# A decoder layer in float32 on one core: TensorE's moving operands read in turn from two halves

## The chip, the cores and the metric

The kernel runs on one core of a Trainium2 chip. The metric is the device time of one execution in microseconds (us); before the change the median of three runs is 2019.43 us (2018.99 to 2019.73). The engines of the core work side by side and wait for each other through semaphores: TensorE (PE in the profile; its weight loads are shown as PEld), VectorE (DVE), ScalarE (ACT), GpSimd (POOL) and SyncE (SP), which here issues the weights' DMAs.

## The reference

One decoder layer on 256 tokens, model width 2048, in float32. Both branches read the same normalized input, and a gated sum of them is projected and added to `x`; a convolutional FFN follows.

```
h = rmsnorm(x, attn_norm_w[l])
proj = h @ w_in[l]
z, xbc, dt_raw, q, k, v, g = split(proj)              # 2048 -> 4096, 6144, 64, 3 x 2048, 4096
y_ssm  = ssd_mixer(z, xbc, dt_raw, ...) @ w_ssm_out   # conv of 4 tokens, 64 heads of 64, 8 groups, state 128
y_attn = moba_attention(q, k, v, ...) @ w_attn_out    # 16 heads of 128; one block of 256, so causal attention
g_ssm, g_attn = split(sigmoid(g + b_gate))
x = x + (g_ssm * y_ssm + g_attn * y_attn) @ w_out
h = rmsnorm(x, ffn_norm_w[l])
u = causal_dwconv(h @ w_up[l], ffn_conv_w, ffn_conv_b)  # 2048 -> 2 x 5632, conv of 3 tokens
u_gate, u_up = split(u)
x = x + (silu(u_gate) * u_up) @ w_down[l]
```

## The kernel before

All weights (about 95 million numbers) are read once from HBM, 1 MB at a time (`unit`, a tile of 128 x 2048 named `wraw`, three buffers, SyncE's queue). To keep float32 accuracy each operand of a product is split into two parts: the high part, rounded to the type float32r that TensorE takes, and the low part, the rest. ScalarE makes the high part of the weights (`whi`, L182), VectorE the low one (`wlo`, L183); each 1 MB gives two such pairs of 128 x 1024. Activations are kept split likewise, transposed, with the channels on the partitions and the 256 tokens in the free dimension: `hp` (input of attention and its gates), `hn` (normalized input of the SSD branch), `ot` (attention output), `yt` (SSD output), `mt` (merged), `fh` (FFN input), `a` (FFN middle). Each is a tile of 128 x 2 x 16 x 256; index 0 and 1 of the second dimension are high and low part.

A product takes three matmuls for each 128 x 128 piece of the weights: high weight with high activation (L215), high weight with low activation (L216), low weight with high activation (L218). This is `cm_chunk`; `cm_unit` makes one output block of 128 channels x 256 tokens out of 48 such matmuls, in one PSUM tile `mm` of four. The weights are the stationary operand, which TensorE loads anew for each matmul; the activation's 256 columns are the moving operand, streamed through. Only the value projection has it the other way round (`tm_chunk`, L376, L377, L382: `hp` is stationary, 512 columns of the weights `wv` move), since values are needed with the tokens on the partitions. Its weights are laid out by `_tm` on the host.

The stages in order: values and `hp` (`tm_units`); queries and keys of 16 heads in pairs, with attention between them (`attn_pair`); attention gates (`gate_attn`, L614) and attention output (L672); the SSD branch in eight groups (`group_units`, then `core_steps`, of which `ydot` has the matmuls L840 and L841 with moving tile `mhl`, and the reads L843, L845, L846 of their PSUM tile `cc`), SSD gates (`gate_ssm`) and SSD output projection (`out_unit`, added up in `yacc`, L894 and L896, a part of `slotA`); merging (`merge`, L947); output projection (L976 to L978); FFN up (`up`, L1013 reads PSUM) and down (`down`, L1038) in three parts. The attention and SSD steps of vectors are spread among the matmul units by `Spread.tick`: a unit's matmuls, then some steps. TensorE's order is that in which the code is written; the other engines' order follows the code as well. Smaller things on TensorE are sums over partitions (L287, L325), transposes (L544 to L546, L793), scores and B-C products (L228 to L230, L515, L516) and probabilities with values (L561 to L564).

The tiles of the split activations begin at addresses that padding tiles (`pad0`, `pad1` and others) set.

Of the kernel before, what the change touches and what calls it, by code (L numbers as in the profile page):

```python
# [8 lines left out]
F32 = mybir.dt.float32  # L9
# [54 lines left out]


def _tm(w, c0, n):
    v = w[:, c0:c0 + n * 512].reshape(4, 4, 128, n, 512).transpose(3, 0, 2, 1, 4)
    return np.ascontiguousarray(v).reshape(n, 4, 128, 2048)


# [50 lines left out]

class Spread:
# [34 lines left out]
def _body(tc, nc, d, out):  # L161
# [48 lines left out]

    def cm_chunk(ps, part, xh, xl, k0, nk, first, last):
        hi, lo = part
        for k in range(nk):
            w = hi[:, k * 128:(k + 1) * 128]
            PE.matmul(ps, w, xh[:, k0 + k], start=first and k == 0, stop=False)  # L215
            PE.matmul(ps, w, xl[:, k0 + k], start=False, stop=False)  # L216
        for k in range(nk):
            PE.matmul(ps, lo[:, k * 128:(k + 1) * 128], xh[:, k0 + k], start=False, stop=last and k == nk - 1)  # L218

    def cm_unit(src, xh, xl, nk=16):  # L220
        parts = unit(src, nk * 128)
# [148 lines left out]
    def tm_chunk(pst, part, k0, first, last):  # L370
        hi, lo = part
        for k in range(2):
            wh = hi[:, k * 512:(k + 1) * 512]
            for tt in range(2):
                ts = slice(tt * 128, (tt + 1) * 128)
                PE.matmul(pst[tt], hph[:, k0 + k, ts], wh, start=first and k == 0, stop=False)  # L376
                PE.matmul(pst[tt], hpl[:, k0 + k, ts], wh, start=False, stop=False)  # L377
        for k in range(2):
            wl = lo[:, k * 512:(k + 1) * 512]
            for tt in range(2):  # L380
                ts = slice(tt * 128, (tt + 1) * 128)
                PE.matmul(pst[tt], hph[:, k0 + k, ts], wl, start=False, stop=last and k == 1)  # L382


    def tm_units(srcs, after_unit, before=None, mid=None):
# [58 lines left out]
    def attn_pair(j):  # L444
        st = {}

        def evac(key, h, ps):
            if h == 0:
                st["n" + key] = ap.tile([128, 2, T], F32, name="n" + key, bufs=2)
                st["s" + key] = ap.tile([128, 2, T], F32, name="sq", bufs=2)  # L450
            S.activation(st["s" + key][:, h], ps, AF.Square)
            S.activation(st["n" + key][:, h], ps, AF.Copy, scale=sm("qn") if key == "q" else kscale)

        def sums(key):
            def f():
# [154 lines left out]
    def gate_attn(o, pg=None):  # L610
        if pg is None:
            pg = cm_unit(d["wga"][o], hph, hpl)
        g = gate_half(o)
        V.tensor_tensor(g, pg, rb, op=MUL)  # L614
        if o >= 6:
            gate_sigmoid(o, g)
        return g
# [22 lines left out]
    def hn_steps():  # L640
        xr = {}

        def load(c):
            def f():
                xr[c] = xb.tile([128, 4, T], F32, name="xr", bufs=2)
                nc.gpsimd.dma_start(xr[c], d["xT"][:, 4 * c:4 * c + 4])
            return f

        def norm(c):
            def f():  # L650
                x = xr.pop(c)
                for k in range(4):
                    V.scalar_tensor_tensor(x[:, k], x[:, k], sm("attn_w", 4 * c + k), rb, op0=MUL, op1=MUL)
                ks = slice(4 * c, 4 * c + 4)
                S.activation(hnh[:, ks], x, AF.Copy)
                V.tensor_tensor(hnl[:, ks], x, hnh[:, ks].bitcast(F32), op=SUB)
            return f

        return [[load(0), load(1)], [], [norm(0), load(2)], [], [norm(1), load(3)], [], norm(2), [], norm(3)]

    sp.add(hn_steps(), 18)
    for o in range(KT):
        if o > 6:
            gl[o] = gate_attn(o)
            sp.tick()
        elif o < 6:
            gate_sigmoid(o, gl[o])
        if o == 3:
            gl[6] = gate_attn(6, pg6)
        po = cm_unit(d["wao"][o], oh_, ol_)  # L670
        g = gl.pop(o)
        V.tensor_tensor(g, g, po, op=MUL)  # L672
        if o % 2:
            nc.gpsimd.dma_start(ma[o // 2], gpair.pop(o // 2))
        sp.tick()
# [19 lines left out]
    def dt_unit():  # L695
        raw = base.tile([128, 2048], F32, name="wraw", bufs=3)
        nc.sync.dma_start(raw[:, :1024], d["wdt"])
        rv = raw[:, :1024].rearrange("p (k c) -> p k c", c=64)
        ps = mm_tile()[:, :T]
        for c in range(2):  # L700
            w = base.tile([128, 1024], F32R, name="whi", bufs=3).rearrange("p (k a c) -> p k a c", a=2, c=64)
            ks = slice(8 * c, 8 * c + 8)
            S.activation(w[:, :, 0], rv[:, ks], AF.Copy)
            V.tensor_tensor(w[:, :, 1], rv[:, ks], w[:, :, 0].bitcast(F32), op=SUB)
            for k in range(8):
                wk = w[:, k].rearrange("p a c -> p (a c)")
                PE.matmul(ps, wk, hnh[:, 8 * c + k], start=c == 0 and k == 0, stop=False)
                PE.matmul(ps, wk, hnl[:, 8 * c + k], start=False, stop=c == 1 and k == 7)
        return ps

    def dt_steps(ps):
# [48 lines left out]
    def core_steps(g):  # L760
# [73 lines left out]
        def ydot(p):  # L834
            def f():
                m = st.pop(("m", p))
                for h in range(2):
                    ps = c_tile().rearrange("p (a t) -> p a t", t=T)
                    x0, x1 = [st["x"][:, s, p, 2 * h:2 * h + 2].rearrange("p a c -> p (a c)") for s in range(2)]
                    PE.matmul(ps, x0, m[:, :, h, 0:256], start=True, stop=False)  # L840
                    PE.matmul(ps[:, :, 128:], x1, m[:, :, h, 256:384], start=False, stop=True)  # L841
                    rs, ls = slice(h * 64, (h + 1) * 64), slice(64 - h * 64, 128 - h * 64)
                    V.scalar_tensor_tensor(yz[rs, p], pr[rs, 4 + p], sm("ssm_d", 4 * g + p, 1, rs), ps[rs, 0],  # L843
                                           op0=MUL, op1=ADD)
                    V.tensor_tensor(yz[rs, p], ps[rs, 1], yz[rs, p], op=ADD)  # L845
                    V.tensor_tensor(yz[rs, p], ps[ls, 0], yz[rs, p], op=ADD)  # L846
                if p % 2:
                    V.tensor_tensor(yz[:, p - 1:p + 1], yz[:, p - 1:p + 1], pr[:, p - 1:p + 1], op=MUL)
            return f
# [32 lines left out]
    def out_unit(q, u, done):  # L882
        parts = unit(d["wso"][q, u])
        yh, yl = yt[:, q % 2, 0], yt[:, q % 2, 1]
        ps = mm_tile()
        for c in range(2):
            cm_chunk(ps[:, c * T:(c + 1) * T], parts[c], yh, yl, 0, 8, True, True)
        done(u, ps.rearrange("p (a t) -> p a t", t=T))

    def acc_done(q):  # L890
        def f(u, ps):
            y = yacc[:, 2 * u:2 * u + 2]
            if q == 0:
                S.activation(y, ps, AF.Copy)  # L894
            else:
                V.tensor_tensor(y, ps, y, op=ADD)  # L896
        return f
# [37 lines left out]
    def merge(u, ps):  # L935
        os_ = slice(2 * u, 2 * u + 2)
        if u < 4:
            g = gate_pool.tile([128, 2, T], F32, name="g", bufs=3)
            nc.gpsimd.dma_start(g, gs[u])
            late = pre[0][:, 2 * u:2 * u + 2]  # L940
            with tc.issue_after(last_rsq[0].ins):
                S.activation(late, late, AF.Sigmoid)
        else:
            g = pre[0][:, 2 * u - 8:2 * u - 6]
        a = gate_pool.tile([128, 2, T], F32, name="g", bufs=3)
        nc.gpsimd.dma_start(a, ma[u])
        V.tensor_tensor(yacc[:, os_], ps, yacc[:, os_], op=ADD)  # L947
        V.tensor_tensor(yacc[:, os_], yacc[:, os_], g, op=MUL)
        V.tensor_tensor(a, yacc[:, os_], a, op=ADD)
        S.activation(mh_[:, os_], a, AF.Copy)  # L950
        V.tensor_tensor(ml_[:, os_], a, mh_[:, os_].bitcast(F32), op=SUB)
# [21 lines left out]
            yield o, pss[o] if o < 2 else cm_unit(d["wout"][o], mh_, ml_)  # L973

    for o, ps in out_products():
        V.tensor_tensor(x1[:, o], ps, x1[:, o], op=ADD)  # L976
        S.activation(fh[:, o], x1[:, o], AF.Copy, scale=sm("ffn_w", o))
        V.scalar_tensor_tensor(fl[:, o], x1[:, o], sm("ffn_w", o), fh[:, o].bitcast(F32), op0=MUL, op1=SUB)  # L978
        if o == 0:
            S.activation(ssum, x1[:, o], AF.Square)  # L980
        else:
# [45 lines left out]
    def down(th):  # L1027
        at = acts[th]
        n = thirds[th][1]
        for o in range(KT):  # L1030
            ps = cm_unit(d[wd[th]][o], at[:, 0], at[:, 1], n)
            if th == 2 and o == KT - 1:
                for h, q in enumerate((S, nc.sync)):
                    hs = slice(h * 128, (h + 1) * 128)
                    V.tensor_tensor(x1[:, o, hs], ps[:, hs], x1[:, o, hs], op=ADD)
                    q.dma_start(out[o][:, hs], x1[:, o, hs])
                continue
            V.tensor_tensor(x1[:, o], ps, x1[:, o], op=ADD)  # L1038
            if th == 2:
                S.dma_start(out[o], x1[:, o])  # L1040

# [29 lines left out]
```

## Time and profile before

| | |
|---|---|
| median of three runs | 2019.43 us (2018.99 to 2019.73) |
| profiled execution, from first to last instruction | 2017.6 us |
| TensorE busy | 2012.3 us, 17203 matmuls |
| VectorE busy | 1496.5 us |
| ScalarE busy | 1189.5 us |
| DMA | 402.40 MB, mean 199 GB/s |

The profiled execution's own time is known as its span alone; the median of the runs is 1.8 us above it. In the profile's rows the columns are, for groups of instructions: line, engine, operation, output tile and inputs, shape, count, then busy time in us, mean duration of one in ns, and the idle time before them. For rows in order of time: start in us, duration in us, engine, line, operation, count in a row. Durations of matmuls overlap, so what one costs is read from the distance of starts.

### The profile page before, as it was taken

Reading aid. Unit: us, or ns where it says so; the run is one execution under the profiler, and the core shown is the slowest. Engines: PE = TensorE matmul, PEld = TensorE weight load, DVE = VectorE, ACT = ScalarE, POOL = GpSimd, SP = SyncE. Lnnn points to the kernel's source line nnn. Section 1 sums busy time; section 2 is a strip of 40 time slices with the busy share of each in tenths; the row PEclk is TensorE's granted clock in tenths of the full one; section 3 lists DMA queues with packets and bytes.
Section 4 is the critical chain, followed back from the end, with each engine's and each line's share of the span. In section 5 each row is a group of like instructions: output and inputs, shape, how many; then the busy total and the mean of one; then the engine's idle time right before and its main releaser. Section 6 shows DMA issues by size and latency. Waiting matters only on the chain.

```text
span 2017.6 us, 40769 instructions
## 1 busy us (share of the span) xinstructions
PE 2012.3 (100%) x17203; PEld 1989.1 (99%) x17203; DVE 1496.5 (74%) x2214; ACT 1189.5 (59%) x1640; POOL 79.0 (4%) x100
## 2 busy tenths in 40 slices
PE   9999999999999999999999999999999999999999
PEld 7999999999999999999999999999999999999999
DVE  7588877656788798888989886677777765677554
ACT  6466655544768867667677645565555553455333
POOL 0012210000000000000000000000000000000000
PEclk9999999999999999999999999999999999999999
DMA  7555555656556555555565575555555555555555
GB/s 290 188 187 183 181 177 206 234 204 215 188 192 217 205 199 208 194 196 190 196 208 178 197 276 200 190 189 198 199 189 191 201 194 189 194 201 190 190 186 169
DMA packets 64351, 402.40 MB, mean 199 GB/s; under 512 B 7655, under 2 KB 10264, under 8 KB 20648
## 3 DMA queue, kind: packets, MB, share of 16 engines
q1 hardware_dynamic: 55384, 376.56, 52.9%
q0 software_dynamic: 5760, 18.97, 3.1%
q10 hardware_dynamic: 3024, 4.27, 0.6%
q8 instruction: 134, 2.20, 0.4%
q14 instruction: 49, 0.40, 0.1%
HBM read 394.44 MB, written 5.33 MB: 198 GB/s over the span
## 4 chain that ended last, share of the span: by engine, by line
PE 99%; DVE 0%; DMA 0%; issue 0%; SPq 0%; ACT 0%; DVEq 0%
PE mm L215 31%; PE mm L218 31%; PE mm L216 31%; PE mm L382 1%; PE mm L376 1%; PE mm L377 1%; PE cc L840 1%; PE cc L841 0%; PE cc L793 0%; DMA wraw<-wv 0%; PE cc L228 0%; PE cc L229 0%; PE cc L230 0%; PE cc L561 0%; DVE wlo L183 0%; DVE xt L318 0%
## 5 line engine op out<-in xcount | busy, mean ns | idle before, releaser
L182 ACT ACTIVATE whi<-wraw 128x1024 fp32r<-128x1024 f32 (+1 forms) x712 | 744.7, 1050 | 664.7 <-PE mm L216 583.2
L183 DVE TENSOR_TENSOR wlo<-wraw,whi 128x1024 fp32r<-128x1024 f32 (+1 forms) x712 | 864.1, 1218 | 242.9 <-ACT whi L182 238.0
L215 PE MATMUL mm<-hn,whi 128*128 128x256 f32 x1536 | 358.7, 277 | 0.0
L216 PE MATMUL mm<-hn,whi 128*128 128x256 f32 x1536 | 358.3, 277 | 0.0
L215 PE MATMUL mm<-fh,whi 128*128 128x256 f32 x1408 | 327.9, 277 | 0.0
L216 PE MATMUL mm<-fh,whi 128*128 128x256 f32 x1408 | 327.8, 276 | 0.0
L215 PEld LDWEIGHTS mm<-hn,whi 128*128 128x128 f32 x1536 | 288.4, 188 | 1.5 <-ACT whi L182 0.2
L216 PEld LDWEIGHTS mm<-hn,whi 128*128 128x128 f32 x1536 | 288.5, 188 | 0.1
L215 PEld LDWEIGHTS mm<-fh,whi 128*128 128x128 f32 x1408 | 264.4, 188 | 0.0
L216 PEld LDWEIGHTS mm<-fh,whi 128*128 128x128 f32 x1408 | 264.3, 188 | 0.0
L218 PE MATMUL mm<-hn,wlo 128*128 128x256 f32 x1536 | 205.6, 277 | 0.0
L218 PEld LDWEIGHTS mm<-hn,wlo 128*128 128x128 f32 x1536 | 188.4, 188 | 0.0
L218 PE MATMUL mm<-fh,wlo 128*128 128x256 f32 x1408 | 188.2, 277 | 0.0
L215 PE MATMUL mm<-hp,whi 128*128 128x256 f32 x768 | 180.1, 278 | 0.0
L216 PE MATMUL mm<-hp,whi 128*128 128x256 f32 x768 | 179.2, 277 | 0.0
L218 PEld LDWEIGHTS mm<-fh,wlo 128*128 128x128 f32 x1408 | 172.7, 188 | 0.0
L215 PE MATMUL mm<-a,whi 128*128 128x256 f32 x704 | 164.4, 277 | 0.0
L216 PE MATMUL mm<-a,whi 128*128 128x256 f32 x704 | 164.3, 276 | 0.0
L216 PEld LDWEIGHTS mm<-hp,whi 128*128 128x128 f32 x768 | 144.3, 188 | 0.1
L215 PEld LDWEIGHTS mm<-hp,whi 128*128 128x128 f32 x768 | 144.3, 188 | 0.1
L215 PEld LDWEIGHTS mm<-a,whi 128*128 128x128 f32 x704 | 132.2, 188 | 0.0
L216 PEld LDWEIGHTS mm<-a,whi 128*128 128x128 f32 x704 | 132.2, 188 | 0.0
(308 smaller groups left out, 3244.1 us busy)
## 6 DMA issues: line engine op xcount, KB each, us to landing
wraw<-wup SPq DMA_DIRECT2D x88, 1024.0 KB, 4.8
wraw<-wssd SPq DMA_DIRECT2D x80, 1024.0 KB, 4.9
wraw<-wqk SPq DMA_DIRECT2D x32, 1024.0 KB, 4.8
wraw<-wso SPq DMA_DIRECT2D x32, 1024.0 KB, 4.9
wraw<-wd SPq DMA_DIRECT2D x32, 1024.0 KB, 4.8
wraw<-wga SPq DMA_DIRECT2D x16, 1024.0 KB, 5.0
wraw<-wao SPq DMA_DIRECT2D x16, 1024.0 KB, 5.0
wraw<-wgs SPq DMA_DIRECT2D x16, 1024.0 KB, 4.8
```

What stands on the lines that cost most here:

```text
L182: last_hi[0] = S.activation(hi[:, :n // 2], raw[:, s], AF.Copy)
L183: V.tensor_tensor(lo[:, :n // 2], raw[:, s], hi[:, :n // 2].bitcast(F32), op=SUB)
L215: PE.matmul(ps, w, xh[:, k0 + k], start=first and k == 0, stop=False)
L216: PE.matmul(ps, w, xl[:, k0 + k], start=False, stop=False)
L218: PE.matmul(ps, lo[:, k * 128:(k + 1) * 128], xh[:, k0 + k], start=False, stop=last and k == nk - 1)
L376: PE.matmul(pst[tt], hph[:, k0 + k, ts], wh, start=first and k == 0, stop=False)
L377: PE.matmul(pst[tt], hpl[:, k0 + k, ts], wh, start=False, stop=False)
L382: PE.matmul(pst[tt], hph[:, k0 + k, ts], wl, start=False, stop=last and k == 1)
L840: PE.matmul(ps, x0, m[:, :, h, 0:256], start=True, stop=False)
```

## The change

The 256 columns of a moving operand are no longer read in storage order but in turn from the first and the second half: 0, 128, 1, 129 and so on. TensorE writes its output to PSUM without gaps, so in PSUM the tokens stand in that shuffled order. There are three ways in which the order is made good again. Where PSUM was read by an elementwise instruction, that one now reads every second element (`unmix`) into the two halves of its output (`halves`). Where a whole chain follows (`hn`, `fh`), the stored activation itself is shuffled, so that reading in turn gives the natural order. For the values the host shuffles the weights' columns in `_tm`. In `ydot` the two "halves" are the high and the low part of `mhl`, column by column.

The streams of L215, L216, L218, L376, L377, L382, L707, L708, L840 and L841 are read so. Not changed are the streams of scores, of probabilities with values, of B-C products, transposes and sums. No instruction is added or taken away, and each engine has its instructions in the same order as before, with the tiles at the same addresses. The PSUM output of L841 begins at column 256 of its tile and not at 128 of each half, and L845 reads from its second column on.

```
 def _tm(w, c0, n):
-    v = w[:, c0:c0 + n * 512].reshape(4, 4, 128, n, 512).transpose(3, 0, 2, 1, 4)
+    v = w[:, c0:c0 + n * 512].reshape(4, 4, 128, n, 256, 2).transpose(3, 0, 2, 1, 5, 4)
...
+def mix(x):
+    return x.rearrange("p (a b) -> p b a", a=2)
+def mixed(ps):
+    return ps.rearrange("p (b a) -> p b a", a=2)
+def unmix(ps):
+    return ps.rearrange("p (b a) -> p a b", a=2)
+def halves(x):
+    return x.rearrange("p (a b) -> p a b", a=2)
...
     def cm_chunk(ps, part, xh, xl, k0, nk, first, last):
         hi, lo = part
+        pm = mixed(ps)
         for k in range(nk):
             w = hi[:, k * 128:(k + 1) * 128]
-            PE.matmul(ps, w, xh[:, k0 + k], start=first and k == 0, stop=False)
-            PE.matmul(ps, w, xl[:, k0 + k], start=False, stop=False)
+            PE.matmul(pm, w, mix(xh[:, k0 + k]), start=first and k == 0, stop=False)
+            PE.matmul(pm, w, mix(xl[:, k0 + k]), start=False, stop=False)
         for k in range(nk):
-            PE.matmul(ps, lo[:, k * 128:(k + 1) * 128], xh[:, k0 + k], start=False, stop=last and k == nk - 1)
+            PE.matmul(pm, lo[:, k * 128:(k + 1) * 128], mix(xh[:, k0 + k]), start=False, stop=last and k == nk - 1)
...
     tm_chunk
-                PE.matmul(pst[tt], hph[:, k0 + k, ts], wh, start=first and k == 0, stop=False)
+                PE.matmul(mixed(pst[tt]), hph[:, k0 + k, ts], mix(wh), start=first and k == 0, stop=False)
...
     attn_pair, evac
-            S.activation(st["s" + key][:, h], ps, AF.Square)
+            S.activation(halves(st["s" + key][:, h]), unmix(ps), AF.Square)
...
     gate_attn
-        V.tensor_tensor(g, pg, rb, op=MUL)
+        V.tensor_tensor(halves(g), unmix(pg), halves(rb), op=MUL)
...
     hn_steps, norm
-                S.activation(hnh[:, ks], x, AF.Copy)
-                V.tensor_tensor(hnl[:, ks], x, hnh[:, ks].bitcast(F32), op=SUB)
+                xe_ = x.rearrange("p k (b a) -> p k a b", a=2)
+                h4, l4 = [t[:, ks].rearrange("p k (a b) -> p k a b", a=2) for t in (hnh, hnl)]
+                S.activation(h4, xe_, AF.Copy)
+                V.tensor_tensor(l4, xe_, h4.bitcast(F32), op=SUB)
...
     ydot
-                    ps = c_tile().rearrange("p (a t) -> p a t", t=T)
+                    pt = c_tile().rearrange("p (t a) -> p t a", a=2)
+                    ps = pt.rearrange("p t a -> p a t")
-                    PE.matmul(ps, x0, m[:, :, h, 0:256], start=True, stop=False)
-                    PE.matmul(ps[:, :, 128:], x1, m[:, :, h, 256:384], start=False, stop=True)
+                    mt = m[:, :, h].rearrange("p a t -> p t a")
+                    PE.matmul(pt, x0, mt[:, 0:256], start=True, stop=False)
+                    PE.matmul(pt[:, 128:], x1, mt[:, 256:384], start=False, stop=True)
...
     out_unit
-        done(u, ps.rearrange("p (a t) -> p a t", t=T))
+        done(u, ps.rearrange("p (o b a) -> p o a b", o=2, a=2))
...
     the output projection
-        V.tensor_tensor(x1[:, o], ps, x1[:, o], op=ADD)
-        S.activation(fh[:, o], x1[:, o], AF.Copy, scale=sm("ffn_w", o))
+        V.tensor_tensor(halves(x1[:, o]), unmix(ps), halves(x1[:, o]), op=ADD)
+        S.activation(halves(fh[:, o]), unmix(x1[:, o]), AF.Copy, scale=sm("ffn_w", o))
...
     down
-                    V.tensor_tensor(x1[:, o, hs], ps[:, hs], x1[:, o, hs], op=ADD)
+                    V.tensor_tensor(x1[:, o, hs], unmix(ps)[:, h], x1[:, o, hs], op=ADD)
-            V.tensor_tensor(x1[:, o], ps, x1[:, o], op=ADD)
+            V.tensor_tensor(halves(x1[:, o]), unmix(ps), halves(x1[:, o]), op=ADD)
```

`mm` and `cc` are PSUM tiles; the rows of L672, L896, L947 and of dt's matmuls L707 and L708 change in the same way as those shown.

More of the change, by code (lines that the diff above doesn't have):

```diff
@@ L375, in tm_chunk @@
                 ts = slice(tt * 128, (tt + 1) * 128)
-                PE.matmul(pst[tt], hph[:, k0 + k, ts], wh, start=first and k == 0, stop=False)
-                PE.matmul(pst[tt], hpl[:, k0 + k, ts], wh, start=False, stop=False)
+                PE.matmul(mixed(pst[tt]), hph[:, k0 + k, ts], mix(wh), start=first and k == 0, stop=False)
+                PE.matmul(mixed(pst[tt]), hpl[:, k0 + k, ts], mix(wh), start=False, stop=False)
         for k in range(2):
@@ L381, in tm_chunk @@
                 ts = slice(tt * 128, (tt + 1) * 128)
-                PE.matmul(pst[tt], hph[:, k0 + k, ts], wl, start=False, stop=last and k == 1)
+                PE.matmul(mixed(pst[tt]), hph[:, k0 + k, ts], mix(wl), start=False, stop=last and k == 1)
     def tm_units(srcs, after_unit, before=None, mid=None):
@@ L450, in evac @@
                 st["s" + key] = ap.tile([128, 2, T], F32, name="sq", bufs=2)
-            S.activation(st["s" + key][:, h], ps, AF.Square)
-            S.activation(st["n" + key][:, h], ps, AF.Copy, scale=sm("qn") if key == "q" else kscale)
+            S.activation(halves(st["s" + key][:, h]), unmix(ps), AF.Square)
+            S.activation(halves(st["n" + key][:, h]), unmix(ps), AF.Copy, scale=sm("qn") if key == "q" else kscale)
         def sums(key):
@@ L671, in _body @@
         g = gl.pop(o)
-        V.tensor_tensor(g, g, po, op=MUL)
+        V.tensor_tensor(halves(g), halves(g), unmix(po), op=MUL)
         if o % 2:
@@ L706, in dt_unit @@
                 wk = w[:, k].rearrange("p a c -> p (a c)")
-                PE.matmul(ps, wk, hnh[:, 8 * c + k], start=c == 0 and k == 0, stop=False)
-                PE.matmul(ps, wk, hnl[:, 8 * c + k], start=False, stop=c == 1 and k == 7)
+                PE.matmul(mixed(ps), wk, mix(hnh[:, 8 * c + k]), start=c == 0 and k == 0, stop=False)
+                PE.matmul(mixed(ps), wk, mix(hnl[:, 8 * c + k]), start=False, stop=c == 1 and k == 7)
         return ps
@@ L887, in out_unit @@
             cm_chunk(ps[:, c * T:(c + 1) * T], parts[c], yh, yl, 0, 8, True, True)
-        done(u, ps.rearrange("p (a t) -> p a t", t=T))
+        done(u, ps.rearrange("p (o b a) -> p o a b", o=2, a=2))
     def acc_done(q):
         def f(u, ps):
-            y = yacc[:, 2 * u:2 * u + 2]
+            y = yacc[:, 2 * u:2 * u + 2].rearrange("p o (a b) -> p o a b", a=2)
             if q == 0:
@@ L946, in merge @@
         nc.gpsimd.dma_start(a, ma[u])
-        V.tensor_tensor(yacc[:, os_], ps, yacc[:, os_], op=ADD)
+        y4 = yacc[:, os_].rearrange("p o (a b) -> p o a b", a=2)
+        V.tensor_tensor(y4, ps, y4, op=ADD)
         V.tensor_tensor(yacc[:, os_], yacc[:, os_], g, op=MUL)
@@ L975, in _body @@
     for o, ps in out_products():
-        V.tensor_tensor(x1[:, o], ps, x1[:, o], op=ADD)
-        S.activation(fh[:, o], x1[:, o], AF.Copy, scale=sm("ffn_w", o))
-        V.scalar_tensor_tensor(fl[:, o], x1[:, o], sm("ffn_w", o), fh[:, o].bitcast(F32), op0=MUL, op1=SUB)
+        V.tensor_tensor(halves(x1[:, o]), unmix(ps), halves(x1[:, o]), op=ADD)
+        S.activation(halves(fh[:, o]), unmix(x1[:, o]), AF.Copy, scale=sm("ffn_w", o))
+        V.scalar_tensor_tensor(halves(fl[:, o]), unmix(x1[:, o]), sm("ffn_w", o), halves(fh[:, o].bitcast(F32)),
+                               op0=MUL, op1=SUB)
         if o == 0:
```

## The prediction

> **What bounds the kernel now.** I read the first two parts of the page, then the chain that ended last, then windows of engine time, and last the starts of single matmuls.
>
> ```profile
> span 2017.6 us, 40769 instructions
> PE 2012.3 (100%) x17203; PEld 1989.1 (99%) x17203; DVE 1496.5 (74%) x2214; ACT 1189.5 (59%) x1640; POOL 79.0 (4%) x100
> PEclk9999999999999999999999999999999999999999
> PE mm L215 31%; PE mm L218 31%; PE mm L216 31%; PE mm L382 1%; PE mm L376 1%; PE mm L377 1%; PE cc L840 1%; PE cc L841 0%; PE cc L793 0%; DMA wraw<-wv 0%; PE cc L228 0%; PE cc L229 0%; PE cc L230 0%; PE cc L561 0%; DVE wlo L183 0%; DVE xt L318 0%
> 540.00:1120.00 580.00, 580.00 (x5035) 576.71 (x5033) 504.54 (x743) 419.24 (x584) 19.92 (x37) 1.00 0.57 199
> 1500.00:1700.00 200.00, 200.00 (x1767) 200.00 (x1766) 136.67 (x194) 104.63 (x129) 0.00 (x0) 1.00 0.55 192
> ```
>
> TensorE is never idle, at a granted clock of 1.00, and 93% of the chain is three matmul lines. The two windows give, in this order: length, busy time of TensorE, of its weight loads, VectorE, ScalarE and GpSimd, then clock and DMA. So only one thing can move the time much: the distance from one matmul's start to the next. In the second window it is 200/1767 = 0.1132 us. Starts say the same:
>
> ```profile
> 1003.30 0.28 PE L215 MATMUL mm<-yt,whi 128*128 128x256 f32 x1
> ...
> 1006.02 0.28 PE L215 MATMUL mm<-yt,whi 128*128 128x256 f32 x1
> 64.31 0.39 PE L376 MATMUL mm<-whi,hp 128*128 128x512 f32 x1
> ...
> 67.05 0.39 PE L376 MATMUL mm<-whi,hp 128*128 128x512 f32 x1
> ```
>
> Between the first two rows lie 24 matmuls of 256 columns (16 on the high part of the weights, 8 on the low): 2.72/24 = 113.3 ns each. Between the other two lie 12 of 512 columns: 2.74/12 = 228.3 ns. The 256 further columns cost 115 ns, so what is paid goes with the columns and is no fixed cost of an instruction. The busy time of one matmul (0.28) overlaps the next and says nothing about this.
>
> How far can the distance fall? Two places of the trace show the engine with less to stream.
>
> ```profile
> 43.47 0.19 PEld L325 LDWEIGHTS cc<-ones,xt 128*128 128x128 f32 x1
> 43.92 0.19 PEld L376 LDWEIGHTS mm<-whi,hp 128*128 128x128 f32 x1
> 43.61 0.36 PE L325 MATMUL cc<-ones,xt 128*128 128x1 f32 x2
> 43.83 0.48 PE L287 MATMUL cc<-xsp,onesr 128*128 128x512 f32 x1
> 539.42 1.04 PE L793 MATMUL cc<-small,slotA 128*128 128x128 f32 x8
> L793 PE MATMUL cc<-small,slotA x32: 272/273/274, 539.4 to 1026.1; 128*128 128x128 f32 x32
> ```
>
> The four matmuls of L325 stream one column each, yet each needs its 128x128 weight load. From the second of these loads to the first of L376 there are four steps in 0.45 us (112 ns each), and from the last but one of these matmuls to L287 two steps in 0.22 us (110 ns). With practically nothing streamed the distance is still about 111 ns: I read this as the price of a weight load. Every matmul of the large lines has such a load (17203 beside 17203 in the page). The transposes of L793, eight in 1.04 us of which the last takes 0.273, start 0.767/7 = 109.6 ns apart, the closest row of this trace for matmuls with full loads and full streams; they aren't of the same kind as the large lines, so I hold this a lower end.
>
> **The change part by part.** Instructions, their order on each engine, tile addresses and bytes moved by DMA stay; no queue is passed and no step moves. Three things change.
>
> First, the moving operand of the large lines is read in another order: columns 0, 128, 1, 129 and so on (0, 256, 1, 257 for 512 columns), written to PSUM in a row. How many:
>
> ```profile
> L215 PE MATMUL mm<-hn,whi 128*128 128x256 f32 x1536 | 358.7, 277 | 0.0
> L215 PE MATMUL mm<-fh,whi 128*128 128x256 f32 x1408 | 327.9, 277 | 0.0
> L215 PE MATMUL mm<-hp,whi 128*128 128x256 f32 x768 | 180.1, 278 | 0.0
> L215 PE MATMUL mm<-a,whi 128*128 128x256 f32 x704 | 164.4, 277 | 0.0
> L215 PE MATMUL mm<-yt,whi 128*128 128x256 f32 x512 | 119.4, 277 | 0.0
> L215 PE MATMUL mm<-ot,whi 128*128 128x256 f32 x256 | 59.7, 277 | 0.0
> L215 PE MATMUL mm<-mt,whi 128*128 128x256 f32 x256 | 59.6, 276 | 0.0
> L707 PE MATMUL mm<-hn,whi 128*128 128x256 f32 x16 | 3.7, 276 | 0.0
> L376 PE MATMUL mm<-whi,hp 128*128 128x512 f32 x128 | 50.6, 395 | 0.9 <-ACT whi L198 0.9
> L840 PE MATMUL cc<-mhl,xx 128*128 128x512 f32 x64 | 24.1, 398 | 0.0
> L841 PE MATMUL cc<-mhl,xx 128*128 128x256 f32 x64 | 18.0, 281 | 0.0
> ```
>
> L215 has 5440; L216 and L218 have as many each, and L707 and L708 add 16 each: 16,352 streams of 256 columns. L376, L377 and L382 have 128 each: 384 of 512. No row shows a stream in the new order, so its price is bounded from both sides. Downwards: 109.6 ns gives 16,352 x 3.7 = 60.5 us. With the load of 111.0 as the floor it is 16,352 x 2.3 = 37.6 us. No gain is 113.3. Upwards, the nearest rows are streams of other tiles that already take longer:
>
> ```profile
> 540.41 0.28 PE L229 MATMUL cc<-bcl,bch 128*128 128x256 f32 x1
> ...
> 541.00 0.28 PE L215 MATMUL mm<-hn,whi 128*128 128x256 f32 x1
> 557.34 0.40 PE L840 MATMUL cc<-mhl,xx 128*128 128x512 f32 x1
> ...
> 558.05 0.28 PE L215 MATMUL mm<-hn,whi 128*128 128x256 f32 x1
> ```
>
> Five matmuls of L228 to L230 fill 0.59 us: 118 ns for the same 256 columns, 4.7 more, with the same number of columns and the same clock. So the distance depends on where and how operands are read, not on the arithmetic; that is what makes a gain from a new order possible, and equally a loss. I take 111.0: the stream's surplus over the load goes, and the load binds in its place. That is nearest to the row with the same load and no stream to disturb it. For the 384 wide streams the load isn't the bound; twice 111.0 is 222.0, so 384 x 6.3 = 2.4 us (ends: 0, and 3.5 us by twice 109.6). L840 and L841 take 0.71/2 = 0.355 us a pair against 0.340 for three times 113.3; 64 pairs could give 1 us and I count nothing.
>
> Second, readers of PSUM take every second element, and some writers of activations skip likewise:
>
> ```profile
> L846 DVE TENSOR_TENSOR slotA<-cc,slotA 64x256 f32<-64x256 f32 x64 | 27.0, 422 | 2.0
> L896 DVE TENSOR_TENSOR slotA<-mm,slotA 128x512 f32<-128x512 f32 x16 | 11.0, 686 | 5.9 <-PE mm L218 5.9
> ACT whi L182 <- PE mm L216: 583.2, 476, 2.1
> SPq L175 <- DVE wlo L183: 1466.1, 280, 9.9
> ```
>
> No row shows a step of two. The bound above counts each element twice: 256 more elements cost 686 - 422 = 264 ns. In the SSD stage that is 192 reads of L843, L845 and L846 x 0.264 = 51 us and 16 of L896 x 0.528 = 8 us, 59 us of VectorE against 580 - 504.5 = 75.5 us that it idles in the window 540 to 1120. Elsewhere there are fewer such reads and more idle time. So I count zero on the path; the cover is that idle time, and ScalarE's 583 us of waiting for TensorE to free a weight buffer, which says that the split of the weights runs ahead. A TensorE that is 2% quicker takes some 40 us from this cover. The weights' DMA queue waits 1466 us for VectorE to free raw buffers, and doesn't come late either. Below zero nothing: a skipping read has no fewer elements.
>
> Third, the last reads of PSUM stand on the path: 0.29 us in the row
>
> ```profile
> 2014.48 0.29 DVE x L1035
> ```
>
> and counted twice some 0.3 us at most. I count nothing.
>
> The sum: 37.6 + 2.4 = 40.0 us of the profiled span of 2017.6, so 1977.6; the runs' median, 2019.43, lies 1.8 above the span, and with that 1979.4: I say 1979.
>
> [...]
>
> **The rivals.**
>
> *More than the load allows.* If the 111 ns of L325 are not the price of a load, and the distance falls to that of the transposes, the gain is 60.5 + 3.5 = 64 us: 1955. For it: L793 also loads 128x128 each time. Against: its loads are of another kind, so they may simply be shorter.
>
> *A part of it.* The stream keeps some of its surplus, 112.5 ns: 16,352 x 0.8 = 13 us, about 2006.
>
> *The order means nothing.* 113.3 is what load and stream cost together, whatever the order: 2019. For it: 113.3 (yt) and 113.2 (the second window, other activations) hardly differ, and both are only 2.3 ns above the bare load.
>
> *Every column pays for its own read: slower.* Contiguous columns share something in the read that columns from two halves don't. The least of this kind is the 118 ns above: 16,352 x 4.7 = 77 us, 2096. The most that I can price is half the rate, 228.3 ns for 256 columns, as now for 512: 16,352 x 115.0 = 1880 us, 384 x 228 = 88 us and 64 x 0.355 = 23 us more: 4010. It decides as soon as a shuffled stream takes more than 113.3 ns, since nothing covers TensorE. Against it speaks no row, since none has the new order; the 118 beside 113.3 only shows that reading costs something in contiguous order too.
>
> [...]
>
> *VectorE becomes the bound in the SSD stage.* 59 us more of work in 75 us of idle time, and bursts that don't fit: some 5 to 20 us lost while nothing is won, 2025 to 2040. This needs reads of PSUM at half speed.
>
> **How the numbers follow.** A measurement of this kernel can tell 0.2%, 4 us, from no change. The load as the new floor, 1965 to 2000: 0.40. Below that: 0.16. A smaller gain, 2000 to 2015: 0.10. No change: 0.14. A column that pays for itself: 0.17, half of it near 4010. VectorE: 0.03. So faster 0.66, same 0.14, slower 0.20. I put the faster cases ahead because the surplus of the present order is seen in two rows (113.3 beside 111, 115 beside 109.6 per 256 columns), while the loss has a row of 118 only, of other tiles. The range runs from 1940, below the 1955 of the transposes by another 1 ns for each matmul since the roundings of that row allow it, to 2032, into the VectorE case; outside lie the costly reads and little else. The faster cases alone span 1940 to 2015.
>
> **What the profile after would show.** Right: TensorE busy throughout at clock 1.00, x17203, and 24 starts of L215, L216, L218 in some 2.66 us instead of 2.72 in each stage alike; the wide streams at about 222 ns. A count of 1767 in a 200 us window would become about 1800. Readers of PSUM: L846's successor near 422 ns (0.42), or up to 686 if a step of two is read at half speed; VectorE's share then rises from 74% to some 80%. Wrong: 24 starts in 2.83 us or more (costly reads), unchanged 2.72 (no effect), 2.62 (the load was no floor), or idle gaps of TensorE with VectorE named as what ended them.

## The result and the profile after

The changed kernel takes 1987.85 us (median of 4 runs, 1986.59 to 1988.05), the kernel before 2019.58 us on the same chip (4 runs, 2018.99 to 2022.19). The ratio is 0.9841, with a 95% interval of 0.9827 to 0.9855: 31.7 us, 1.6% faster. The forecast was 1979 us with a range of 1940 to 2032, and its reason was that the stream's surplus over the weight load goes and the load binds in its place.

The first two rows are the page of the changed kernel, the third is its chain that ended last, shares of the span by engine and line. After the change L215, L216 and L218 are L232, L233 and L235, and L376, L377 and L382 are L393, L394 and L399.

```profile
span 1986.2 us, 40773 instructions
PE 1978.8 (100%) x17203; PEld 1961.8 (99%) x17203; DVE 1494.4 (75%) x2214; ACT 1189.3 (60%) x1640; POOL 78.6 (4%) x100
PE mm L232 30%; PE mm L233 30%; PE mm L235 30%; PE mm L399 1%; PE mm L393 1%; PE mm L394 1%; DVE wlo L199 1%; PE cc L861 1%; PE cc L812 0%; PE cc L862 0%; DVE slotA L775 0%; DMA xw<-x 0%; PE cc L245 0%; PE cc L247 0%; PE cc L246 0%
```

The picture is that of before: practically as many instructions, TensorE full, three matmul lines hold 90% of the chain. VectorE's busy time is 1494.4 us where it was 1496.5, and ScalarE's 1189.3 where it was 1189.5. What changed is the distance between starts. The windows have the columns of those shown before; the starts are from the out-projection of the SSD stage and from the values' projection.

```profile
540.00:1120.00 580.00, 578.05 (x5104) 575.48 (x5103) 510.70 (x752) 417.57 (x578) 18.84 (x35) 1.00 0.58 201
1500.00:1700.00 200.00, 200.00 (x1794) 200.00 (x1793) 132.59 (x183) 101.65 (x121) 0.00 (x0) 1.00 0.55 197
```

```profile
988.04 0.28 PE L232 MATMUL mm<-yt,whi 128*128 128x256 f32 x1
...
990.72 0.28 PE L232 MATMUL mm<-yt,whi 128*128 128x256 f32 x1
...
59.71 0.38 PE L393 MATMUL mm<-whi,hp 128*128 128x512 f32 x1
...
62.30 0.38 PE L393 MATMUL mm<-whi,hp 128*128 128x512 f32 x1
```

1794 starts in 200 us are 111.5 ns apart, where 1767 were 113.2. Between the first two starts lie 24 matmuls again: 2.68 us, 111.7 ns each, against 2.72. Between the other two lie 12 wide ones: 2.59 us, 215.8 ns each, against 228.3. From here on I give such a distance as the mean over all matmuls of a kind in a trace, from one start to the next, with the outer 5% at each end left out: 256 columns went from 113.3 or 113.4 to 111.6 or 111.7 ns in every stage, 512 from 229 to 215.8.

The readers, from the groups of instructions (mean ns of one behind the bar):

```profile
L867 DVE TENSOR_TENSOR slotA<-cc,slotA 64x256 f32<-64x256 f32 x64 | 27.0, 422 | 2.0
L917 DVE TENSOR_TENSOR slotA<-mm,slotA 128x512 f32<-128x512 f32 x16 | 11.0, 686 | 4.6 <-PE mm L235 4.6
L674 ACT ACTIVATE hn<-xr 128x1024 fp32r<-128x1024 f32 x4 | 5.5, 1384 | 9.4 <-DVE xr L670 9.4
L999 ACT ACTIVATE fh<-x,small 128x256 fp32r<-128x256 f32 x16 | 9.4, 586 | 3.9 <-DVE x L998 3.9
```

L867 and L917 are L846 and L896 of before, now with a step of two in PSUM: 422 and 686 ns, to the nanosecond as they were. Dearer are only the instructions that skip in SBUF: L674 took 1065 ns before, L999 511, and the VectorE instructions that make the low parts beside them rose by 115 and 30 ns. Their cover held: none of them ends a wait of TensorE.

### The profile page after: what moved, and what is told of

Same layout as the page of the kernel before. It is cut to its first block, busy times and chain, and to the rows that moved or that the text cites. A ratio compares the mean times of both kernels' runs of the same rounds, so it can differ in the third digit from the quotient of the medians.

```text
span 1986.2 us, 40773 instructions
## 1 busy us (share of the span) xinstructions
PE 1978.8 (100%) x17203; PEld 1961.8 (99%) x17203; DVE 1494.4 (75%) x2214; ACT 1189.3 (60%) x1640; POOL 78.6 (4%) x100
## 4 chain that ended last, share of the span: by engine, by line
PE 98%; DVE 2%; issue 0%; ACT 0%; DMA 0%; DVEq 0%; ACTq 0%
PE mm L232 30%; PE mm L233 30%; PE mm L235 30%; PE mm L399 1%; PE mm L393 1%; PE mm L394 1%; DVE wlo L199 1%; PE cc L861 1%; PE cc L812 0%; PE cc L862 0%; DVE slotA L775 0%; DMA xw<-x 0%; PE cc L245 0%; PE cc L247 0%; PE cc L246 0%
## 5 line engine op out<-in xcount | busy, mean ns | idle before, releaser
L198 ACT ACTIVATE whi<-wraw 128x1024 fp32r<-128x1024 f32 (+1 forms) x712 | 742.9, 1049 | 621.9 <-PE mm L233 569.0
L232 PE MATMUL mm<-hn,whi 128*128 128x256 f32 x1536 | 353.3, 275 | 1.9 <-ACT whi L198 1.9
L233 PE MATMUL mm<-hn,whi 128*128 128x256 f32 x1536 | 353.0, 275 | 0.0
L232 PE MATMUL mm<-fh,whi 128*128 128x256 f32 x1408 | 323.6, 275 | 0.0
L233 PE MATMUL mm<-fh,whi 128*128 128x256 f32 x1408 | 323.5, 275 | 0.0
L232 PEld LDWEIGHTS mm<-hn,whi 128*128 128x128 f32 x1536 | 294.9, 192 | 3.0 <-ACT whi L198 2.3
L233 PEld LDWEIGHTS mm<-hn,whi 128*128 128x128 f32 x1536 | 295.0, 192 | 0.1
L233 PEld LDWEIGHTS mm<-fh,whi 128*128 128x128 f32 x1408 | 270.5, 192 | 0.0
L232 PEld LDWEIGHTS mm<-fh,whi 128*128 128x128 f32 x1408 | 270.3, 192 | 0.0
L235 PE MATMUL mm<-hn,wlo 128*128 128x256 f32 x1536 | 202.9, 275 | 0.0
L235 PEld LDWEIGHTS mm<-hn,wlo 128*128 128x128 f32 x1536 | 186.9, 192 | 0.0
L235 PE MATMUL mm<-fh,wlo 128*128 128x256 f32 x1408 | 186.1, 275 | 0.0
L232 PE MATMUL mm<-hp,whi 128*128 128x256 f32 x768 | 177.2, 276 | 0.0
L233 PE MATMUL mm<-hp,whi 128*128 128x256 f32 x768 | 176.5, 275 | 0.0
L235 PEld LDWEIGHTS mm<-fh,wlo 128*128 128x128 f32 x1408 | 171.4, 192 | 0.0
L233 PE MATMUL mm<-a,whi 128*128 128x256 f32 x704 | 162.2, 275 | 0.0
L232 PE MATMUL mm<-a,whi 128*128 128x256 f32 x704 | 162.2, 275 | 0.0
L232 PEld LDWEIGHTS mm<-hp,whi 128*128 128x128 f32 x768 | 147.5, 192 | 0.1
L233 PEld LDWEIGHTS mm<-hp,whi 128*128 128x128 f32 x768 | 147.5, 192 | 0.1
L233 PEld LDWEIGHTS mm<-a,whi 128*128 128x128 f32 x704 | 135.3, 192 | 0.0
L232 PEld LDWEIGHTS mm<-a,whi 128*128 128x128 f32 x704 | 135.2, 192 | 0.0
```

The lines of the kernel that those rows point to most:

```text
L198: last_hi[0] = S.activation(hi[:, :n // 2], raw[:, s], AF.Copy)
L232: PE.matmul(pm, w, mix(xh[:, k0 + k]), start=first and k == 0, stop=False)
L233: PE.matmul(pm, w, mix(xl[:, k0 + k]), start=False, stop=False)
L235: PE.matmul(pm, lo[:, k * 128:(k + 1) * 128], mix(xh[:, k0 + k]), start=False, stop=last and k == nk - 1)
```

## The experiments

**Is it the streams, or what stands around them?** The first kernel keeps the changed layout of inputs and value weights and every changed reader, and gives TensorE its columns in storage order again:

```diff
-        pm = mixed(ps)
+        pm = ps
-            PE.matmul(pm, w, mix(xh[:, k0 + k]), start=first and k == 0, stop=False)
+            PE.matmul(pm, w, xh[:, k0 + k], start=first and k == 0, stop=False)
```

and likewise for the other streams that the change touched. The tokens come out in another order by it; the work is the same.

> The changed kernel with all its skipping readers of PSUM, its shuffled stored inputs and value weights, but every moving operand of TensorE read in storage order again (its output tokens are therefore in another order than the reference's; the work is the same). My theory (the streams' reading pays): 24 starts take 2.72 us again and the time is that of before, 2019.6, within 3 us, since VectorE has 75 us to spare in the SSD stage. Rival (the readers or the layout bring a part of the gain, or cost some of it): a time of 2010 or less, or of 2025 or more.

Measured: 2020.29 us against 2019.86, ratio 1.0001 with an interval of 0.9991 to 1.0011. A window of the FFN products, in its profile:

```profile
1320.00:1640.00 320.00, 320.00 (x2826) 320.00 (x2825) 239.04 (x359) 184.06 (x240) 0.00 (x0) 1.00 0.55 195
```

320/2826 = 113.2 ns, the distance of before. So layout and readers neither gain nor cost, and the whole gain belongs to the order in which TensorE reads.

**Which orders are quick?** In the next kernels the high and low activations of each product are read in a pattern of its own, the first and last stream of each unit staying whole in storage order. A pattern is a list of (step, count) in columns, the innermost last; (1, 256) is storage order, (1, 128), (128, 2) the order of the change. The listings of patterns here and below are shortened from the table in each kernel.

```diff
+    'hp': [(1, 256)],                    'hn': [(1, 2), (2, 128)],
+    'ot': [(1, 64), (64, 4)],            'yt': [(2, 64), (128, 2), (1, 2)],
+    'mt': [(4, 32), (128, 2), (1, 4)],   'fh': [(16, 8), (128, 2), (1, 16)],
+    'a':  [(1, 16), (16, 16)],
```

> Only the order in which TensorE reads the 256 moving columns differs, by activation tile (the outputs are in the wrong token order): hp in storage order; hn all even columns and then all odd ones (steps of 8 bytes); ot four quarters in turn; yt two columns from one half, two from the other; mt four and four; fh sixteen and sixteen; a sixteen passes with steps of 64 bytes. Theory A (a stream pays for reading neighbours in a row): 113.3 ns for hp, about 113 for fh (runs of 64 bytes), falling with shorter runs to 111.7 for yt, ot and a; hn between. Theory B (it only matters that two places are read in turn): mt, yt and fh all 111.7, a and hn 113.3. [...]

Measured: 2881.4 us. The results are of shuffled tokens, which leaves the work as it was. The windows lie, in this order, in the stages of ot (four quarters in turn), hn (even columns, then odd ones), yt (runs of 2 from the two halves), mt (runs of 4), fh (runs of 16) and a (sixteen blocks in turn):

```profile
335.00:375.00 40.00, 40.00 (x283) 40.00 (x282) 27.74 (x40) 18.91 (x19) 4.81 (x8) 1.00 0.62 216
500.00:600.00 100.00, 100.00 (x447) 90.81 (x446) 38.47 (x53) 24.44 (x29) 1.67 (x3) 1.00 0.29 102
1740.00:1810.00 70.00, 70.00 (x431) 70.00 (x430) 40.60 (x48) 23.16 (x25) 4.83 (x9) 1.00 0.57 197
1820.00:1910.00 90.00, 90.00 (x716) 90.00 (x715) 53.01 (x75) 45.28 (x62) 0.00 (x0) 1.00 0.50 175
1930.00:2280.00 350.00, 350.00 (x2919) 350.00 (x2919) 247.06 (x371) 189.45 (x247) 0.00 (x0) 1.00 0.52 184
2600.00:2870.00 270.00, 270.00 (x1256) 253.16 (x1255) 73.79 (x89) 55.57 (x59) 0.00 (x0) 1.00 0.28 97
```

Length over count gives 141, 224, 162, 126, 120 and 215 ns; the altered streams alone (without the two whole ones of each unit) are at 143, 229, 167, 126, 120 and 220, and hp in storage order at 113 to 114. No other order is even as quick as storage order, and both theories' tables fall. The costly reads that the prediction held possible do exist, at twice the price, but for other orders than the one that the change uses.

**Does the spacing of the two halves matter?** The pattern stays (1, 128), (d, 2); only d varies, so that other columns are read than the product needs:

```diff
+    'hp': d = 4,  'hn': d = 16,  'yt': d = 64,  'mt': d = 132,
+    'fh': d = 256,  'a': d = 512,  'ot': d = 1024,
```

> TensorE reads two runs of 128 columns in turn, as in the change, but the second run begins at another distance from the first, by activation tile (the outputs are wrong): hp 16 bytes, hn 64, yt 256, mt 528, fh 1024, a 2048, ot 4096; the change itself has 512. Theory A (two reads in a row from different places are enough): 111.7 ns for all from 64 bytes on, hp like storage order, 113.3. Rival (the distance decides, because some places share a path): distances differ by over 0.5 ns from each other, the multiples of 512 alike and mt (528) different; L862, whose halves lie 3072 bytes apart and which takes 109.1, says that 109 is possible at some distance.

Measured: 1992.94 us, and in each of the seven stages 111.66 to 111.68 ns for the altered streams, from two columns 16 bytes apart to 4096. Windows in the stages of hp (16 bytes) and a (2048):

```profile
75.00:95.00 20.00, 20.00 (x181) 20.00 (x180) 10.21 (x10) 10.37 (x16) 0.00 (x0) 1.00 0.57 200
1850.00:1970.00 120.00, 120.00 (x1072) 120.00 (x1072) 63.06 (x76) 47.97 (x51) 0.00 (x0) 1.00 0.60 199
```

Theory A had hp at 113.3, like storage order; it isn't. No effect of the distance between addresses shows here.

**Is 111.67 the stream or the load?** The weight load is cut to 64 columns (hp, hn), 32 (fh, a) or 96 (yt, mt), with the stream of 256 columns in storage order for the first of each pair and in turn for the second; ot keeps a whole load and storage order. The products of the weight columns beyond that are left out. In short, beside the line of the changed kernel:

```diff
-            PE.matmul(pm, w, mix(xh[:, k0 + k]), start=first and k == 0, stop=False)
+            PE.matmul(shaped(ps[:W, :n], counts), w[:, :W], ap, start=start, stop=stop)
```

> The weight loads of the large lines are made narrower (fewer stationary columns, so a part of the output channels isn't computed), with the stream of 256 columns in storage order or taken in turn: hp 64 columns loaded, storage order; hn 64, in turn; fh 32, storage order; a 32, in turn; yt 96, storage order; mt 96, in turn; ot 128, storage order. Theory S (the stream in storage order pays by itself, and what the change leaves, 111.7, is the weight load): storage order stays at 113.3 with any load, in turn falls to 109 or less with a narrower load. Theory L (stream and load get in each other's way): storage order falls with the width, to about 111 at 64 and 110 at 32, and in turn falls as well.

Measured: 2019.12 us. Windows in the stages of mt (96, in turn), fh (32, storage order) and a (32, in turn):

```profile
1210.00:1280.00 70.00, 70.00 (x641) 70.00 (x640) 47.16 (x67) 40.37 (x55) 0.00 (x0) 1.00 0.57 202
1300.00:1640.00 340.00, 340.00 (x2914) 314.14 (x2913) 247.62 (x372) 189.61 (x247) 0.00 (x0) 1.00 0.53 189
1880.00:2010.00 130.00, 130.00 (x1189) 129.57 (x1187) 70.70 (x86) 52.91 (x56) 0.00 (x0) 1.00 0.57 193
```

109.2, 116.7 and 109.3 ns. In turn, the distance falls to 109.13 ns with 32, 64 and 96 columns alike: I take that as the bare stream of 256 columns. In storage order a smaller load gains nothing, so there the load isn't what is paid for, and the last 2.5 ns of the changed kernel belong to the load of 128 columns. What neither theory had: in storage order the distance even rises with a smaller load, to 115.9 (hp), 116.7 (fh) and 117.3 ns (yt), while ot with its whole load stays at 113.3. No run shows why.

For streams read in turn two prices are thus measured: 109.13 ns for 256 columns here, and 215.8 for the 512 columns of the changed kernel's wide streams. In storage order this kernel paid 113.3 and 229.

**The load by itself.** The reverse test: loads whole, streams shortened. The products of the columns that aren't streamed are left out.

```diff
+    'hp': [(1, 128)],            'hn': [(1, 64), (128, 2)],   'fh': [(1, 192)],
+    'a':  [(1, 96), (128, 2)],   'yt': [(1, 64)],   'mt': [(1, 32), (128, 2)],
+    'ot': [(1, 112), (128, 2)],
```

> The weight loads stay whole (128 columns each); the streams of each activation are shortened, so most products are left out: hp 128 columns in storage order, hn 128 in turn, fh 192 in storage order, a 192 in turn, yt 64 in storage order, mt 64 in turn, ot 224 in turn. Theory L (the 111.67 ns of the changed kernel is the price of a 128-column weight load, and no stream takes part in it): all seven come to 110.8 to 111.8 ns, whatever their length and order, and the total stays near 1985 us. [...] Theory D (the distance is a sum of stream and a fixed part): 64 columns at about 30 ns, 128 at 57, total far below 1500 us.

Measured: 2366.47 us, far from what any theory gave for the total. Windows in the stages of hp (128), hn (128), mt (64), fh (192) and a (192); the clock is the third number from the end:

```profile
75.00:95.00 20.00, 20.00 (x181) 20.00 (x180) 10.11 (x11) 10.27 (x17) 0.00 (x0) 1.00 0.56 201
500.00:580.00 80.00, 78.94 (x376) 78.80 (x375) 30.21 (x37) 22.71 (x25) 1.66 (x3) 0.51 0.36 126
1490.00:1640.00 150.00, 150.00 (x705) 150.00 (x704) 52.11 (x75) 43.15 (x59) 0.00 (x0) 0.50 0.30 106
1700.00:1990.00 290.00, 290.00 (x2593) 290.00 (x2592) 218.14 (x328) 161.39 (x219) 0.00 (x0) 1.00 0.56 199
2220.00:2360.00 140.00, 140.00 (x1251) 140.00 (x1251) 72.81 (x89) 54.54 (x58) 0.00 (x0) 1.00 0.56 189
```

Where the clock was 1.00, the altered streams stand at 111.62 (hp), 111.67 (fh) and 111.66 ns (a), whatever their length and order: theory L. D is out altogether, and a price that grows with the streamed columns doesn't show either: 128 give no less than 192. But with 64 columns streamed per load the granted clock fell to 0.50, and the distance there is 213 ns; with hn's 128 it fell for a part of the stage, to 0.51 in the row above, though it held at 1.00 for hp's 128. That is where the total went, and how many columns would keep the clock isn't shown. The single steps show two prices and hardly anything between: of hn's streams 71% stand at 111.6 ns and 27% at 213.3, of yt's with 64 columns 16% and 79%. I read these as the two clocks, so that where the clock was full 64 columns too leave the price of the load. TensorE is never idle in the row of mt (150.00 of 150.00 us) and has a clock of 0.50 there; by what rule the clock is granted isn't shown.

**More orders.** Patterns chosen to find what two in turn has that the others lack (some read columns twice or leave some out):

```diff
+    'hp': [(64, 2), (128, 2), (1, 64)],  'hn': [(1, 42), (42, 6)],  'fh': [(2, 128), (1, 2)],
+    'a': [(2, 128), (256, 2)],  'yt': [(1, 32), (32, 8)],  'mt': [(1, 128), (1, 2)],
+    'ot': [(1, 128), (2, 2)],
```

> Each activation's stream of 256 columns is read in another order, results are of wrong columns, readers stay. Theory N (what is quick is that the innermost run has just two elements, wherever they lie): a, every second column of two blocks 1024 bytes apart in turn, 111.7 ns; ot, two reads 8 bytes apart (columns 0, 2, 1, 3), 111.7; mt, neighbours that overlap (0, 1, 1, 2), 111.7; yt, eight blocks of 32 in turn, and hn, six of 42 in turn, at least the 143 of four in turn; hp, runs of 64 in turn, between 113.3 and the 120 of runs of 16; fh, pairs that make up storage order, 111.7 by the form of the pattern or 113.3 if only addresses count. Theory A (each of two readers must itself go through consecutive addresses): as N but a at about 220 to 229, as other steps of two, and fh at 113.3. Theory B (addresses of consecutive columns must lie in different 16-byte groups): a, yt and hn 111.7, ot and mt 113 or more. In all, 2000 to 2350 us, the more the slower eight in turn is.

Measured: 2315.55 us; hp 113.95 ns, hn 146.6, fh 113.32, a 113.32, yt 220.0, mt 111.68, ot 111.67. Windows in the stages of yt, mt and a:

```profile
1400.00:1500.00 100.00, 100.00 (x474) 93.49 (x473) 46.83 (x58) 27.92 (x32) 4.85 (x9) 1.00 0.43 150
1510.00:1590.00 80.00, 80.00 (x718) 80.00 (x716) 52.48 (x76) 45.24 (x61) 0.00 (x0) 1.00 0.55 198
2170.00:2310.00 140.00, 140.00 (x1237) 140.00 (x1237) 71.79 (x87) 53.70 (x57) 0.00 (x0) 1.00 0.55 185
```

Theory B falls at yt (eight blocks in turn, 220) and at mt and ot (2 reads a few bytes apart, yet quick). N and A fall at a: a step of two within each half costs neither nothing nor 220 but 1.7 ns. What stands is a table: two reads in turn, each going on by one column, are quick at every spacing tried, from 4 bytes to 4096; four, six (252 columns), eight and sixteen in turn take 143, 147, 220 and 220 ns. Why two in turn beat storage order isn't settled by these runs.

**Is the load's price in reading its columns?** Streams as in the changed kernel; the 128 columns of a weight load are read with a step, so that other columns of the weights enter than the product needs:

```diff
+STEP = {'hp': 2, 'hn': 4, 'fh': 6, 'a': 3, 'yt': 5, 'mt': 1, 'ot': 2}
```

> Streams are read in turn as in the changed kernel; the 128 columns of each weight load are read with a step: hp 2, hn 4, fh 6, a 3, yt 5, mt 1 (as now), ot 2; the weights are thus wrong ones. Theory L1 (the load binds, and its price is in reading its columns as the stream's is): the distance goes from 111.7 to about 220 where the step is 2 or more, as streams with a step of 2 did (229 for 256 columns), mt stays 111.7, total near 3600 us. Theory L2 (the load binds, but its price is in moving weights into the array and not in reading them): all 111.7, total 1988 us. Theory L3 (half of the reading is hidden): 113 to 180, more with larger steps.

Measured: 3302.05 us; mt (step 1) 111.68 ns, hp and ot (2) 118.3, a (3) 175, hn (4) 235, yt (5) 224, fh (6) 225. Windows in the stages of hp, mt and a:

```profile
75.00:95.00 20.00, 20.00 (x172) 20.00 (x170) 9.94 (x10) 9.48 (x14) 0.00 (x0) 1.00 0.49 178
1920.00:1990.00 70.00, 70.00 (x627) 70.00 (x626) 46.36 (x67) 40.09 (x55) 0.00 (x0) 1.00 0.56 198
3070.00:3290.00 220.00, 220.00 (x1276) 220.00 (x1275) 75.53 (x92) 56.69 (x60) 0.00 (x0) 1.00 0.36 124
```

Nothing but the load changed, and the distance follows its step, from 111.68 ns at 1 to 235 at 4; L2, by which the reading costs nothing, is out. L1 had 220 for every step from 2 on, which holds from 4 (224 to 235); a step of 2 costs 6.6 ns, one of 3 already 63. That the 111.67 of step 1 is the price of reading too isn't shown: another limit of the load at 111.67, passed by the reading from step 2 on, would look the same.

**A version that uses this.** If 111.67 belongs to the load and 215.8 for 512 columns to the stream, one load for two streams of 256 saves what the two loads cost over the stream. In the output projection and both FFN products (mt, fh, a) one matmul of 512 columns takes the high activations in turn, then the low ones in turn. In the new function for these stages, beside the lines that it stands in for:

```diff
-            PE.matmul(pm, w, mix(xh[:, k0 + k]), start=first and k == 0, stop=False)
-            PE.matmul(pm, w, mix(xl[:, k0 + k]), start=False, stop=False)
+            both = bass.AP(tensor=xh.tensor, offset=xh[:, k0 + k].offset,
+                           ap=[list(xh.ap[0]), [xl.offset - xh.offset, 2], [1, 128], [128, 2]])
+            PE.matmul(two, hi[:, k * 128:(k + 1) * 128], both, start=first and k == 0, stop=False)
```

`two` is a whole PSUM tile of 512 columns; its readers add the two halves.

> A full version: in the output projection and both FFN products (mt, fh, a) the high weights are loaded once for one stream of 512 columns, the high part of the activations in turn and then the low part in turn, into the two halves of a PSUM tile; the low weights add to the first half; readers add the two halves (one more DVE addition for mt and a, one ScalarE copy and one more addition for fh). 256 + 1408 + 704 = 2368 pairs of matmuls become one. Theory W (the changed kernel's distance of 111.67 is its load, the stream alone is 109.1, and a wide stream in turn takes 215.8): each pair takes 215.8 in place of 223.3, a gain of 7.5 x 2368 = 18 us, total 1970 us. Theory V (half the loads gone gives nothing, since 111.67 belongs to the stream): 1988 us. Theory R (readers of two halves come too late for the four PSUM tiles): TensorE waits at the ends of units, 1990 to 2010 us. Theory P (three-level patterns read at the slow rate, 143 ns and more for 256 columns): 2080 us or more.

Measured: 1971.11 us (4 runs, 1969.73 to 1971.39) against 2019.16, ratio 0.976 with an interval of 0.9743 to 0.9776: theory W's 1970. (The 1987.85 of the changed kernel had a ratio of 0.9841.) Its page, the FFN window, and two starts in the up-projection:

```profile
span 1969.6 us, 36276 instructions
PE 1961.4 (100%) x14835; PEld 1880.5 (95%) x14835; DVE 1555.2 (79%) x2367; ACT 1201.9 (61%) x1728; POOL 78.5 (4%) x100
```

```profile
1300.00:1600.00 300.00, 300.00 (x1834) 275.43 (x1833) 256.77 (x404) 186.22 (x288) 0.00 (x0) 1.00 0.59 201
```

```profile
1399.76 1.89 PE L243 MATMUL mm<-fh,whi 128*128 128x512 f32 x8
...
1402.38 1.89 PE L243 MATMUL mm<-fh,whi 128*128 128x512 f32 x8
```

Eight wide streams and eight narrow ones take 2.62 us, where 24 narrow ones take 2.68. TensorE still never waits in the window; VectorE's added 61 us stay in its idle time. This kernel beats both others.

## Why the prediction was right, point by point

*The mechanism* was as said: the stream's surplus goes, the load binds, TensorE stays full at clock 1.00 with its 17203 matmuls, and the distance falls in every stage alike. The two experiments on load and stream show it from both sides: a smaller load brings 109.13, a smaller stream leaves 111.6 to 111.7.

*The main term* was mis-sized. Counted on were 2.3 ns for each of 16,352 streams, 37.6 us; in the two profiles the mean distance of these streams, without the steps over 130 ns at waits and seams (12 before, 16 after), fell from 113.43 to 111.66, so 29.0 us. The step that failed is the floor of 111.0: four steps read off rows printed to 10 ns can't fix it to better than 1 or 2 ns, and 0.7 ns are 11 us here.

*The wide streams* were taken at twice the load, 222.0. They have one load for 512 columns, so the load doesn't bind them, and nothing makes them two loads long: 215.8, 384 x 13.3 = 5.1 us in place of 2.4. L861 and L862 (L840 and L841 before), counted at nothing, gave 64 x 26.5 ns = 1.7 us.

*Not foreseen* was a loss of some 4.4 us: 29.0 + 5.1 + 1.7 is 35.8, and the spans differ by 31.4. So the 40.0 forecast lost 8.6 on the main term and 4.4 here, and gained 2.7 and 1.7 on the two small terms; that these two make up for the loss is luck. The first place is the start of TensorE, before and then after:

```profile
5.82 0.50 PE L376 MATMUL mm<-whi,hp 128*128 128x512 f32 x1 [0.55 <-ACT whi L198]
...
9.27 0.39 PE L376 MATMUL mm<-whi,hp 128*128 128x512 f32 x1
```

```profile
5.97 0.79 PE L393 MATMUL mm<-whi,hp 128*128 128x512 f32 x1 [0.70 <-ACT whi L214]
...
6.98 0.63 PE L393 MATMUL mm<-whi,hp 128*128 128x512 f32 x1
7.41 0.63 PE L394 MATMUL mm<-whi,hp 128*128 128x512 f32 x1
...
10.76 0.38 PE L393 MATMUL mm<-whi,hp 128*128 128x512 f32 x1
```

In this execution the first streams start 0.43 us apart, half rate, and the 13th at 10.76 us instead of 9.27: 1.5 us behind where 0.2 ahead was due. With the same streams at the start, four more profiles begin so (narrow loads among them) and three don't (spacings among them): it comes and goes with the execution. Whether the change makes it likelier isn't shown; the two profiles with these streams in storage order both start at full rate. The granted clock reads 1.00 from 5.50 to 10.50 us, in which these starts lie; what halves their rate isn't shown.

The second is a new wait in the SSD stage, rows of ScalarE and TensorE:

```profile
661.54 1.28 ACT L785 ACT_TABLE_LOAD   x1 [1.89 <-DVE slotA L775]
...
666.02 1.28 ACT L927 ACT_TABLE_LOAD   x1
...
669.09 0.38 PE L232 MATMUL mm<-hn,whi 128*128 128x256 f32 x1 [1.60 <-ACT whi L198]
```

ScalarE waits 1.89 us for VectorE, loads a table, runs a long activation and loads a second table, and its next weight split comes 1.6 us late: the step from start to start is 1.87 us there in place of 0.11. At the same place in the kernel before, ScalarE waited 0.42 us for VectorE and TensorE not at all. VectorE is all but full on the way there, with 11.91 us of work between 653.0 and 665.3 us; I read the wait as a lead that a quicker TensorE has used up, since such a VectorE can't follow it. The same step is 1.89 us long in the profile of the last experiment and 1.65 in that of the spacings; the two profiles with all streams in storage order don't have it. 0.5 us went the same way at 587 us. The prediction had drawn this cover from totals, ScalarE's 583 us of waiting (569.0 after) and VectorE's idle time in the stage: a total doesn't tell where the cover is thin. The start, these two and a wait at 37 us for a low part (a step of 1.00 us in place of 0.68) make up 4.2 of the 4.4 us.

*The readers* at nothing: right, and by more than argued. The bound of 59 us for VectorE counted each skipped element twice; a step of two in PSUM costs nothing (422 and 686 ns, as before).

*The rivals.* "More than the load allows" (1955) and "a part of it" (2006) are out by 111.67 as the price that a load leaves with any shorter stream; "the order means nothing" by 2020.29 against 1987.85 with all else alike. "Every column pays for its own read" had its price right and is wrong for this order: 220 to 229 ns for other patterns of four-byte columns, but 111.66 to 111.68 ns for two runs in turn at seven spacings from 16 to 4096 bytes. "VectorE becomes the bound" needed reads at half speed, and there were none; but its bursts that don't fit are, by the reading above, what the 1.6 us came from.

## What to carry to other kernels

Where TensorE is full, measure the distance between starts, and find by a smaller load and by a smaller stream which of the two it is (with the granted clock in view: with streams of 64 columns it fell to 0.50 here); the rest is that number times the count. For streams of float32r (fp32r in the rows), read two runs in turn, each going on by one column (111.7 ns here beside 113.4), and try no other order without timing it (up to 229 ns here); where the load then binds, give one load a stream of 512 columns (1971.11 us here beside 1987.85). Read a floor off hundreds of starts and not off four, and look for the thinnest cover in each stage and not for the total.

## What was not expected of the hardware

- Two reads in turn are quicker than storage order (109.13 beside 116 to 117 ns with small loads), and the spacing from 16 to 4096 bytes makes no difference (111.66 to 111.68), while four to sixteen in turn took 143 to 220 ns.
- Storage order isn't steady: in the profiled execution of the first experiment (2028.49 us, above its median) two thirds of ot's streams, a quarter of hp's and a sixth of hn's took 116 ns or more, about 118, where fewer than one in twenty did before. Streams of 256 columns read in turn beside whole loads stood at 111.6 to 111.7 in every stage of the changed kernel and of the spacings.
- A weight load read with a step of 2 costs 6.6 ns, with 3 it costs 63, with 4 to 6 some 113 to 123.
- TensorE issuing back to back with 64 columns for each load of 128 was granted a clock of 0.50; with 128 columns it was 1.00 in one stage and 0.51 in a part of another.
